# Four conditioning chunks of the second mixer move from TensorE to VectorE, and four are made during the first feed-forward stage

## The chip, the core and the metric

The kernel runs on one NeuronCore of a Trainium2 chip. The core has five engines with instruction streams of their own: TensorE (PE in the profile; PEld is its weight load), VectorE (DVE), ScalarE (ACT), GpSimd (POOL) and SyncE (SP), which here only issues DMAs. Each engine works through its stream in order and waits on semaphores for the others. The metric is the device time of one execution in microseconds (us): 676.04 us for the kernel before, the median of 3 runs (675.55 to 677.71).

## The reference

Two layers (L = 2) work on 256 tokens of width 1024 in float32. In each layer a conditioning vector c gives, through a matrix of 1024 x 6144, a shift, a scale and a gate for the mixer and the same for the feed-forward part:

```python
c_act = jax.nn.silu(c)
for l in range(DEPTH):
    mod = (c_act @ w_ada[l] + b_ada[l])[:, None, :]
    shift_a, scale_a, gate_a, shift_f, scale_f, gate_f = jnp.split(mod, 6, axis=-1)
    h = rmsnorm(x, g_mix_pre[l]) * (1.0 + scale_a) + shift_a
    y = hybrid_mixer(h, w_in[l], ...)           # three kinds of attention, then w_out
    x = x + gate_a * rmsnorm(y, g_mix_post[l])
    h = rmsnorm(x, g_ffn_pre[l]) * (1.0 + scale_f) + shift_f
    x = x + gate_f * rmsnorm(swiglu(h, w_gate_up[l], w_down[l]), g_ffn_post[l])
```

The conditioning is a product of one vector with a matrix: 48 MB of weights for both layers, and little arithmetic. Everything else is matrix products over 256 tokens, and row norms and softmaxes between them.

## The kernel before

**Stages.** The program runs mixer 0, feed-forward 0, mixer 1, feed-forward 1. Between two of them lies a boundary: the post-norm of one stage and the pre-norm of the next, token tile by token tile (two tiles of 128 tokens, t = 0 and 1). In a boundary ScalarE squares and sums a row (`junk`), VectorE adds the sums (`rs`), GpSimd takes the power -1/2, VectorE scales (`yg`, `x`, `xn`), TensorE transposes (`xT`), ScalarE applies scale and shift (`hv`, line 384), and VectorE splits the result into a leading part (`h1aH`, line 386) and a rest (`h1aL`, line 387).

**Products.** Every product is made of three, of leading parts and rests. So each weight piece of 128 x 1024 is loaded (`raw`, four buffers), rounded by ScalarE (`wh`, line 102) and subtracted by VectorE (`wl`, line 103; six buffers of each).

**Conditioning.** For each of the four norms there are 12 chunks of 256 columns: chunks 0 to 7 hold shift and scale of 128 features each (`scale_step`), and four more the gates (`gate_step`). A chunk is 1 MB, loaded in two halves (`adaw`, line 257) into a ring of four half buffers, so that the load of a half waits until the half four places earlier has been used. A chunk is made in one of two ways (`ada_chunk`): on VectorE, by one multiply-and-sum instruction for each half (line 266, shown as CUSTOM_DVE in the trace), or on TensorE, by 8 products (`adap`, line 274), a copy by ScalarE (`adasb`, line 277), two transposes (`adac`, line 286) and a sum by VectorE (line 287). `on_dve` says which. For the second norm of layer 1 (`ab11`) VectorE takes chunks 1, 3, 5 and 7, and TensorE takes 0, 2, 4 and 6.

**Where chunks stand.** `todo` is a list of such steps, and `fill()` takes the next one off it. Mixer 1 has 12 steps (4 gates, 8 scales), called from its start, from its latents and after each of its eight pairs of heads. Feed-forward 0 has 12 steps (4 gates of its own, 8 scales for the first norm of layer 1), one for each tile f of the hidden width from f = 4 on (f runs from 0 to 21). In the feed-forward stage a chunk is also ordered behind the weight piece before it (`order_after`).

**What sets the order.** The tile framework places each engine's instructions by a model of durations and priorities when the program is built, so an instruction can stand far from where it is written: in the kernel before, the loads of mixer 1's gates and of its scale chunks 0 to 2 are issued, and the gates and chunk 1 made, before feed-forward 0 has ended. On the chip that order is fixed. All loads go through SP's one queue: a load that waits for its buffer holds up every load behind it.

Of the kernel before, what the change touches and what calls it, by code (L numbers as in the profile page):

```python
# [14 lines left out]
L = 2  # L15
D = 1024
# [17 lines left out]
MIX_DVE = (3, 5, 6, 7), (1, 3, 5, 7)  # L34


def on_dve(l, which, j):
    """which engine takes the products of a chunk (j < 8: scale and shift, then gates) with the conditioning"""
    if which == 1 and j < KC:
        return j in MIX_DVE[l]  # L40
    return j >= KC or l > 0
# [3 lines left out]
def block_kernel(ctx, tc, A, out):  # L45
# [47 lines left out]
    def chain(i):  # L93
        """products of the start: in the order in which they are written"""
# [10 lines left out]
    def prep(key):  # L105
# [14 lines left out]
        for u in range(nh):  # L120
# [8 lines left out]
            # beside the norms of the layer boundary: small pieces, so that a norm waits less  # L129
# [16 lines left out]
    def mm3(ps, w, x, start, stop):  # L146
        # weights stationary
# [4 lines left out]
    def tokens(ps, h, ts_, w, halves=False):  # L152
        """one token tile over all of D, w: (high, low) per chunk"""
# [4 lines left out]
        # the low parts of h arrive last  # L158
# [9 lines left out]
    def mm3t(ps, x, w, start, stop):  # L168
        # tokens stationary
# [10 lines left out]
    # columns: per norm and chunk b_ada of shift, b_ada of scale (32) | 32:40 g_mix_pre | 40:48 g_ffn_pre  # L180
    #          48:50 g_q_lat | 50:51 g_kv_lat | 51:59 g_group
    #          59:91 per norm b_ada of the gate, g_mix_post | g_ffn_post
# [17 lines left out]
    # the tensor engine's clock is up by the time that the first weights arrive  # L200
# [4 lines left out]
    # silu(c), repeated over 32 columns  # L205
# [8 lines left out]
    # and as a row on every partition  # L214
# [8 lines left out]
    # T5 bias of the causal tile, as a Toeplitz read of the per-distance values  # L223
    mobab = const.tile([P, 4, S], F32, name="mobab")

    def t5_bias():
# [12 lines left out]
        # a copy for each partition: row p is read from its element 127 - p on  # L239
# [20 lines left out]
    def ada_chunk(l, which, j):  # L260
        raws = loaded.pop((l, which, j), None) or ada_load(l, which, j)
        if on_dve(l, which, j):
            # features on partitions
# [16 lines left out]
    def ada_columns(l, which, j, sb, dst):  # L280
        """sums of a chunk, features on partitions"""
# [17 lines left out]
    def rows_of(sb, tag):  # L299
        """the columns of sb as one row on every partition, through a scratch in DRAM"""  # L300
# [29 lines left out]
    def scale_step(l, which, kc, sb=None):  # L330
        if kc == 0:
            ABs[l, which] = act.tile([P, KC, 2], F32, tag="ab", bufs=3, name=f"ab{l}{which}")
        ada_scale(l, which, ABs[l, which], kc, ada_chunk(l, which, kc) if sb is None else sb)

# [502 lines left out]
    def ffn(l, hH, hL, norm, fill, silu_set):  # L837
# [63 lines left out]
        for f in range(NF):  # L901
            if f >= HEADF:
# [3 lines left out]
                if f >= 4:  # L906
                    fill()
# [207 lines left out]
```

## Time and profile before

| what | value |
|---|---|
| runs | 676.04 us median of 3 (675.55 to 677.71) |
| profiled execution, span from first to last instruction | 675.6 us |
| TensorE busy | 639.2 us (95%) |
| VectorE busy | 451.4 us (67%) |
| ScalarE busy | 366.5 us (54%) |
| GpSimd busy | 51.3 us (8%) |
| moved by DMA | 155.29 MB, mean 230 GB/s |
| conditioning halves made by VectorE (line 266) | 64, 77.7 us |

The page has no time of the profiled execution other than its span, which lies within 0.1 us of the fastest run and 0.4 us below the median. Feed-forward 0 lies at about 176 to 350 us, the boundary to mixer 1 at 350 to 367 us, mixer 1 at 367 to 470 us. Busy shares of the whole span say little here: what counts is which engine the others wait for in each of these stretches, and where TensorE has gaps.

### The profile page before, as it was taken

Reading aid. Unit: us, or ns where it says so; the run is one execution under the profiler, and the core shown is the slowest. Engines: PE = TensorE matmul, PEld = TensorE weight load, DVE = VectorE, ACT = ScalarE, POOL = GpSimd, SP = SyncE. Lnnn points to the kernel's source line nnn. Section 1 sums busy time; section 2 is a strip of 40 time slices with the busy share of each in tenths; the row PEclk is TensorE's granted clock in tenths of the full one; section 3 lists DMA queues with packets and bytes.
Section 4 is the critical chain, followed back from the end, with each engine's and each line's share of the span. In section 5 each row is a group of like instructions: output and inputs, shape, how many; then the busy total and the mean of one; then the engine's idle time right before and its main releaser. Section 6 shows DMA issues by size and latency. Waiting matters only on the chain.

```text
span 675.6 us, 12108 instructions
## 1 busy us (share of the span) xinstructions
PE 639.2 (95%) x4543; PEld 565.5 (84%) x4543; DVE 451.4 (67%) x969; ACT 366.5 (54%) x758; POOL 51.3 (8%) x90
## 2 busy tenths in 40 slices
PE   8989759999999999999999999899899999999996
PEld 6878647667999999999978988668799999999994
DVE  2458277888777777798658765775878755555543
ACT  5447427768654444444458665786764444444431
POOL 1000021421000000000001010240100000000000
PEclk9999979999999999999999999899999999999999
DMA  9968595886478898898844875551558676555511
GB/s 320 407 227 286 168 322 179 281 289 215 147 245 316 310 328 304 313 337 290 313 139 147 296 230 184 201 182 64 187 195 276 219 236 184 185 181 185 184 62 63
DMA packets 44410, 155.29 MB, mean 230 GB/s; under 512 B 5136, under 2 KB 6464, under 8 KB 44352
## 3 DMA queue, kind: packets, MB, share of 16 engines
q1 hardware_dynamic: 44352, 154.52, 67.4%
q8 instruction: 36, 0.59, 0.3%
q14 instruction: 22, 0.18, 0.1%
HBM read 152.64 MB, written 1.86 MB: 229 GB/s over the span
## 4 chain that ended last, share of the span: by engine, by line
PE 74%; DVE 9%; DMA 8%; ACT 3%; issue 2%; POOL 2%; SPq 1%; DVEq 0%; POOLq 0%; ACTq 0%
PE gu L148 11%; PE gu L149 11%; PE gu L150 11%; PE y L171 8%; PE y L172 8%; PE y L170 8%; DMA adaw<-in_w_ada_dram 4%; DVE wl L103 3%; PE adap L274 2%; PE o L478 2%; DMA scr<-band 2%; ACT wh L102 1%; DMA raw_b<-in_w_b_dram 1%; POOL rs L343 1%; DVE adaw L266 1%
## 5 line engine op out<-in xcount | busy, mean ns | idle before, releaser
L103 DVE TENSOR_TENSOR wl<-raw_gu,wh 128x1024 fp32r<-128x1024 f32 (+1 forms) x100 | 108.5, 1096 | 68.8 <-ACT wh L102 68.5
L102 ACT ACTIVATE wh<-raw_gu 128x1024 fp32r<-128x1024 f32 (+1 forms) x100 | 94.4, 958 | 92.6 <-PE gu L149 64.5
L148 PE MATMUL gu<-h0fL,wh 128*128 128x256 f32 x304 | 86.2, 283 | 0.0
L148 PE MATMUL gu<-h1fL,wh 128*128 128x256 f32 x304 | 86.2, 283 | 0.0
L149 PE MATMUL gu<-h1fH,wh 128*128 128x256 f32 x304 | 86.0, 283 | 0.0
L149 PE MATMUL gu<-h0fH,wh 128*128 128x256 f32 x304 | 86.0, 283 | 0.0
L150 PE MATMUL gu<-h0fH,wl 128*128 128x256 f32 x304 | 86.0, 283 | 0.0
L150 PE MATMUL gu<-h1fH,wl 128*128 128x256 f32 x304 | 86.0, 283 | 0.0
L266 DVE CUSTOM_DVE_ANT_0 adaw<-adaw,crow 128x1024 f32<-128x1024 f32 x64 | 77.7, 1229 | 8.4 <-DMA adaw<-in_w_ada_dram 8.4
L102 ACT ACTIVATE wh<-raw_dn 128x1024 fp32r<-128x1024 f32 x44 | 46.7, 1062 | 56.8 <-issue 34.7
L171 PE MATMUL y<-wh,hid 128*128 128x512 f32 x176 | 69.6, 396 | 0.0
L170 PE MATMUL y<-wh,hid 128*128 128x512 f32 x176 | 69.5, 396 | 0.0
L172 PE MATMUL y<-wl,hid 128*128 128x512 f32 x176 | 69.5, 395 | 0.0
L103 DVE TENSOR_TENSOR wl<-raw_dn,wh 128x1024 fp32r<-128x1024 f32 x44 | 53.7, 1224 | 23.3 <-ACT wh L102 23.1
L149 PEld LDWEIGHTS gu<-h0fH,wh 128*128 128x128 f32 x304 | 58.3, 192 | 0.4
L149 PEld LDWEIGHTS gu<-h1fH,wh 128*128 128x128 f32 x304 | 58.3, 192 | 0.4
L148 PEld LDWEIGHTS gu<-h1fL,wh 128*128 128x128 f32 x304 | 58.2, 192 | 0.4
L148 PEld LDWEIGHTS gu<-h0fL,wh 128*128 128x128 f32 x304 | 58.2, 192 | 0.4
L150 PEld LDWEIGHTS gu<-h1fH,wl 128*128 128x128 f32 x304 | 58.3, 192 | 0.0
L150 PEld LDWEIGHTS gu<-h0fH,wl 128*128 128x128 f32 x304 | 58.3, 192 | 0.0
L343 POOL TENSOR_TENSOR rs<-rs,mhalf 128x1 f32<-128x1 f32 x16 | 11.0, 687 | 439.1 <-DVE rs L342 439.1
L172 PEld LDWEIGHTS y<-wl,hid 128*128 128x128 f32 x176 | 33.0, 188 | 8.0
(331 smaller groups left out, 1483.1 us busy)
## 6 DMA issues: line engine op xcount, KB each, us to landing
adaw<-in_w_ada_dram SPq DMA_DIRECT2D x96, 512.0 KB, 6.6
raw_gu<-in_w_gu_dram SPq DMA_DIRECT2D x88, 512.0 KB, 4.7
raw_dn<-in_w_dn_dram SPq DMA_DIRECT2D x44, 512.0 KB, 4.7
raw_out<-in_w_out_dram SPq DMA_DIRECT2D x16, 512.0 KB, 5.0
raw_b<-in_w_b_dram SPq DMA_DIRECT2D x12, 512.0 KB, 5.7
raw_a<-in_w_a_dram SPq DMA_DIRECT2D x8, 448.0 KB, 10.0
raw_uq<-in_w_uq_dram SPq DMA_DIRECT2D x4, 512.0 KB
raw_vm<-in_w_vm_dram SPq DMA_DIRECT2D x4, 512.0 KB, 5.0
```

What stands on the lines that cost most here:

```text
L102: ACT.activation(dst_h, src, AF.Copy)
L103: return DVE.tensor_tensor(dst_l, src, dst_h.bitcast(F32), op=ALU.subtract)
L148: chain(PE.matmul(ps, w[0], x[1], start=start, stop=False))
L149: chain(PE.matmul(ps, w[0], x[0], start=False, stop=False))
L150: chain(PE.matmul(ps, w[1], x[0], start=False, stop=stop))
L170: PE.matmul(ps, x[1], w[0], start=start, stop=False)
L171: PE.matmul(ps, x[0], w[0], start=False, stop=False)
L172: PE.matmul(ps, x[0], w[1], start=False, stop=stop)
L266: i = DVE.tensor_tensor_reduce(out=raws[u], in0=raws[u], in1=crow, op0=ALU.mult, op1=ALU.add, scale=1.0, scalar=0.0, accum_out=sb[:, u:u + 1])
L274: chain(PE.matmul(ps[32 * g:32 * g + 32, :], crep[:, kc, :], raws[kc // 4][:, g * 256:(g + 1) * 256], start=kc < 4, stop=kc >= 4, tile_pos ...
L343: POOL.tensor_tensor(r, r, mhalf, op=ALU.pow)
L478: PE.matmul(o[64 * u:64 * u + 64, lo:lo + P], v[:, u * 64:(u + 1) * 64], ps[u][:, i * P:(i + 1) * P], start=start, stop=stop, tile_positio ...
```

## The change

`on_dve` now answers yes for every chunk of layer 1, so chunks 0, 2, 4 and 6 of the second norm leave TensorE; the host lays out their weights for VectorE. Chunks 0 to 3 (`FFN_MADE`) leave the list of mixer 1 and are appended to that of feed-forward 0, behind the 12 steps that it had. Feed-forward stages call `fill()` from f = 3 on and not from f = 4. `scale_step` makes its result tile at the first chunk it meets and not at chunk 0. Comments and docstrings were dropped as well, so that line numbers shift by 2 (line 266 becomes 268, 103 becomes 105); those lines of the diff are left out here.

```diff
-MIX_DVE = (3, 5, 6, 7), (1, 3, 5, 7)
+MIX_DVE = 3, 5, 6, 7
+
+FFN_MADE = 0, 1, 2, 3
 
 def on_dve(l, which, j):
-    if which == 1 and j < KC:
-        return j in MIX_DVE[l]
+    if l == 0 and which == 1 and j < KC:
+        return j in MIX_DVE
     return j >= KC or l > 0
...
     def scale_step(l, which, kc, sb=None):
-        if kc == 0:
+        if (l, which) not in ABs:
             ABs[l, which] = act.tile([P, KC, 2], F32, tag="ab", bufs=3, name=f"ab{l}{which}")
...
                 up(f)
                 while turns:
                     turns.pop(0)()
-                if f >= 4:
+                if f >= 3:
                     fill()
...
-        todo += [(gate_step, l, 0, j) for j in range(4)] + [(scale_step, l, 1, j) for j in range(KC)]
+        todo += [(gate_step, l, 0, j) for j in range(4)]
+        todo += [(scale_step, l, 1, j) for j in range(KC) if l == 0 or j not in FFN_MADE]
...
         if l + 1 < L:
             todo.extend((scale_step, l + 1, 0, j) for j in range(KC))
+            todo.extend((scale_step, l + 1, 1, j) for j in FFN_MADE)
```

VectorE's stream at the end of feed-forward 0 and the start of the boundary, before: `hid` is the rest of the last hidden tile, `yg` and `rs1` the post-norm of token tile 0.

```order
L103 TENSOR_TENSOR hid_1936<-ffv_3950,hid_1936 128x256
L405 TENSOR_TENSOR yg_4125<-y_2503,gp_2689 128x512
L342 TENSOR_SCALAR rs1_4133<-s2_4127 128x1
L405 TENSOR_TENSOR yg_4126<-y_2504,gp_2689 128x512
L411 SCALAR_TENSOR_TENSOR x_75<-yg_4125,rs1_4133,x_75 128x512
```

The same place in the changed kernel; adaw_4629 and adaw_4630 are the halves of chunk 4, adaw_4789 is the first half of chunk 5 (the ISA row after each is the read of its sum).

```order
L105 TENSOR_TENSOR hid_1936<-ffv_3987,hid_1936 128x256
L268 ISA adaw_4629,adasum_4633<-adaw_4629,crow_110 128x1024
L268 ISA adasum_4633 128x1
L268 ISA adaw_4630,adasum_4633<-adaw_4630,crow_110 128x1024
L268 ISA adasum_4633 128x1
L407 TENSOR_TENSOR yg_4162<-y_2512,gp_2622 128x512
L296 TENSOR_TENSOR ab11_3444<-adasum_4633,first_73 128x2
L298 SCALAR_TENSOR_TENSOR ab11_3444<-ab11_3444,first_73 128x1
L268 ISA adaw_4789,adasum_4793<-adaw_4789,crow_110 128x1024
L268 ISA adasum_4793 128x1
L344 TENSOR_SCALAR rs1_4170<-s2_4164 128x1
L407 TENSOR_TENSOR yg_4163<-y_2513,gp_2622 128x512
```

Three halves now stand between the last hidden tile and the first `rs1` of the norm, where there were none.

VectorE's stream in the pre-norm of token tile 0, before, with `yg` and `rs1` of token tile 1 behind it:

```order
L386 CAST h1aH_4075<-hv4_4154 128x4x128
L387 TENSOR_TENSOR h1aL_4076<-hv4_4154,h1aH_4075 128x4x128
L386 CAST h1aH_4075<-hv4_4168 128x4x128
L387 TENSOR_TENSOR h1aL_4076<-hv4_4168,h1aH_4075 128x4x128
L405 TENSOR_TENSOR yg_4175<-y_2511,gp_2689 128x512
L342 TENSOR_SCALAR rs1_4183<-s2_4177 128x1
```

The same place in the changed kernel; adaw_4790 is the second half of chunk 5.

```order
L388 CAST h1aH_4112<-hv4_4191 128x4x128
L268 ISA adaw_4790,adasum_4793<-adaw_4790,crow_110 128x1024
L268 ISA adasum_4793 128x1
L389 TENSOR_TENSOR h1aL_4113<-hv4_4191,h1aH_4112 128x4x128
L388 CAST h1aH_4112<-hv4_4205 128x4x128
L407 TENSOR_TENSOR yg_4212<-y_2520,gp_2622 128x512
L389 TENSOR_TENSOR h1aL_4113<-hv4_4205,h1aH_4112 128x4x128
L344 TENSOR_SCALAR rs1_4220<-s2_4214 128x1
```

A half stands between leading part and rest of the first four feature tiles, which the first product of mixer 1 reads.

TensorE's stream in mixer 1 ahead of the third pair of heads, before: `qkp` is a projection, `kn` and `qp` are keys and queries of the pair, and `adap` and `adac` make chunk 2.

```order
L150 MATMUL qkp_4862<-h1aH_4075,wl_4449 128x256
L274 MATMUL adap_4916<-adaw_4912,crep_108 32x256 x4
L274 MATMUL adap_4916<-adaw_4913,crep_108 32x256 x4
L148 MATMUL kn_4933<-kvL_4081,wh_4103 128x256
L149 MATMUL kn_4933<-kvH_4080,wh_4103 128x256
L150 MATMUL kn_4933<-kvH_4080,wl_4104 128x256
L148 MATMUL qp_4939<-cqL_4083,wh_4087 128x256
L149 MATMUL qp_4939<-cqH_4082,wh_4087 128x256
L150 MATMUL qp_4939<-cqH_4082,wl_4088 128x256
L148 MATMUL qp_4939<-cqL_4083,wh_4095 128x256
L286 MATMUL adac_4927<-first_73,adasb_4925 128x128 x2
L149 MATMUL qp_4939<-cqH_4082,wh_4095 128x256
```

The same place in the changed kernel:

```order
L152 MATMUL qkp_4886<-h1aH_4112,wl_4486 128x256
L150 MATMUL kn_4945<-kvL_4118,wh_4140 128x256
L151 MATMUL kn_4945<-kvH_4117,wh_4140 128x256
L152 MATMUL kn_4945<-kvH_4117,wl_4141 128x256
L150 MATMUL qp_4951<-cqL_4120,wh_4124 128x256
L151 MATMUL qp_4951<-cqH_4119,wh_4124 128x256
L152 MATMUL qp_4951<-cqH_4119,wl_4125 128x256
L150 MATMUL qp_4951<-cqL_4120,wh_4132 128x256
L151 MATMUL qp_4951<-cqH_4119,wh_4132 128x256
```

The ten instructions are gone and nothing stands in their place; it is the same for the other three chunks.

## Rows read from the trace of the kernel before

**Rows 1.** Windows by stage: us, busy (count) of each engine, clock, DMA.

```profile
core 0: us, PE busy (x) PEld busy (x) DVE busy (x) ACT busy (x) POOL busy (x), PEclk, DMA share, GB/s
176.00:350.00 174.00, 174.00 (x1225) 163.00 (x1225) 132.28 (x217) 80.83 (x115) 0.55 (x1) 1.00 0.82 285
350.00:367.00 17.00, 15.35 (x88) 13.08 (x86) 14.94 (x35) 13.76 (x38) 2.32 (x3) 1.00 0.54 166
367.00:470.00 103.00, 97.88 (x726) 81.97 (x727) 69.28 (x220) 71.93 (x195) 19.08 (x35) 0.98 0.57 191
```

**Rows 2.** The same window for tile adap, then tile adac alone.

```profile
367.00:470.00 103.00, 4.28 (x64) 1.67 (x64) 1.50 (x4) 0.98 0.57 191
367.00:470.00 103.00, 1.64 (x8) 0.86 (x8) 0.66 (x4) 0.98 0.57 191
```

**Rows 3.** Chain that ended last, mixer 1: start us, us, what.

```profile
412.70 1.00 PE adap L274 x16
414.72 0.22 PE adac L286 x2
```

**Rows 4.** Timeline of PE, mixer 1: start, us, form, [idle before <-releaser].

```profile
403.24 0.44 PE L451 MATMUL pt<-first,e 128*128 128x128 f32 x2 [0.39 <-POOL e L445]
...
426.83 0.77 PE L458 MATMUL s<-kx,qx 128*128 128x128 f32 x2 [1.53 <-DVE qx L761]
...
439.54 0.43 PE L478 MATMUL o<-pts,vc 128*64 128x128 f32 x2 [0.38 <-ACT pts L453]
...
447.71 0.50 PE L170 MATMUL y<-wh,o1L 128*128 128x512 f32 x1 [0.87 <-DVE o1L L103]
```

**Rows 5.** Windows of mixer 1 in which the clock fell.

```profile
426.00:428.00 2.00, 1.17 (x4) 1.10 (x5) 2.00 (x4) 1.95 (x5) 0.00 (x0) 0.69 0.35 109
428.00:430.00 2.00, 2.00 (x10) 1.26 (x10) 1.63 (x6) 0.30 (x1) 0.00 (x0) 0.50 0.68 221
```

**Rows 6.** Timeline of DVE, mixer 1: two conditioning halves.

```profile
418.83 1.23 DVE L266 CUSTOM_DVE_ANT_0 adaw<-adaw,crow 128x1024 f32<-128x1024 f32 x1 [2.22 <-DMA adaw<-in_w_ada_dram]
...
443.62 1.36 DVE L266 CUSTOM_DVE_ANT_0 adaw<-adaw,crow 128x1024 f32<-128x1024 f32 x1
```

**Rows 7.** Window of the last pairs of mixer 1.

```profile
436.00:450.00 14.00, 12.33 (x103) 7.64 (x103) 13.93 (x71) 12.47 (x45) 8.34 (x16) 1.00 0.82 279
```

**Rows 8.** Page, group of the conditioning on VectorE.

```profile
L266 DVE CUSTOM_DVE_ANT_0 adaw<-adaw,crow 128x1024 f32<-128x1024 f32 x64 | 77.7, 1229 | 8.4 <-DMA adaw<-in_w_ada_dram 8.4
```

**Rows 9.** Timeline of DVE, end of feed-forward 0 and boundary.

```profile
344.86 0.69 DVE L405 TENSOR_TENSOR yg<-y,gp 128x512 f32<-128x512 f32 x1 [2.65 <-ACT junk L356]
347.72 0.21 DVE L342 TENSOR_SCALAR rs<-s 128x1 f32<-128x1 f32 x1 [2.16 <-ACT junk L356]
...
366.18 0.43 DVE L386 CAST h1aH<-hv 128x512 fp32r<-128x512 f32 x1 [0.64 <-ACT hv L384]
```

**Rows 10.** Windows of the end of feed-forward 0.

```profile
288.00:305.00 17.00, 17.00 (x121) 15.95 (x120) 16.22 (x30) 7.82 (x11) 0.00 (x0) 1.00 0.96 341
305.00:344.00 39.00, 39.00 (x263) 35.88 (x262) 26.35 (x41) 17.61 (x24) 0.00 (x0) 1.00 0.84 294
344.00:350.00 6.00, 6.00 (x27) 4.82 (x26) 2.84 (x6) 2.88 (x7) 0.55 (x1) 1.00 0.02 6
```

**Rows 11.** DMA issues from 312 to 344 us: count, KB each, median us to landing.

```profile
adaw<-in_w_ada_dram SPq DMA_DIRECT2D x6, 512.0 KB, 7.2
```

**Rows 12.** Timeline of PE, boundary and start of mixer 1.

```profile
353.35 1.10 PE L380 MATMUL xT<-first,xn 128*128 128x128 f32 x8 [0.63 <-DVE xn L377]
...
356.92 0.43 PE L170 MATMUL vps<-wh,h1aL 128*128 128x420 f32 x1
...
367.39 0.46 PE L170 MATMUL vps<-wh,h1aL 128*128 128x420 f32 x1 [0.92 <-DVE h1aL L387]
...
386.24 0.33 PE L567 MATMUL latT<-first,lat 128*128 128x128 f32 x1 [0.23 <-DVE kvL L571]
```

**Rows 13.** Timeline of DVE, start of mixer 1.

```profile
381.85 2.55 DVE L103 TENSOR_TENSOR wl<-raw_b,wh 128x512 fp32r<-128x512 f32 x4 [1.31 <-ACT wh L102]
```

## The prediction

> **What bounds the kernel now.** I read the windows by stage first. In feed-forward 0 TensorE is busy for 174.00 of 174 us and VectorE for 132.28 [rows 1]: there the weight products are the bound, and VectorE has 42 us to spare. In mixer 1 TensorE is busy for 97.88 of 103 us; what is not busy lies in gaps that VectorE, ScalarE and GpSimd release [rows 1, 4]. In the boundary between them VectorE is busy for 14.94 of 17 us and TensorE waits for the norm [rows 1, 12]. So an instruction taken from TensorE in mixer 1 counts nearly in full, one added to VectorE in feed-forward 0 counts nothing while it keeps up, and one added to VectorE in the boundary counts wherever it stands in the chain of the norm. All three happen here.
>
> **Taken from TensorE.** The four chunks have 4.28 us of `adap` and 1.64 us of `adac` [rows 2]. Busy times of TensorE overlap, since ends are modelled; the chain of waits counts 1.00 + 0.22 = 1.22 us for one chunk [rows 3], 4.9 us for four. The ends are thus 4.9 and 5.9; I take 5.2, nearer to the chain, which doesn't count overlaps twice. In the order nothing takes the place of these instructions, and the products around them don't wait for the conditioning.
>
> **Taken from VectorE in mixer 1.** The halves of chunks 3, 5 and 7 stand between the softmax instructions there; one waited 2.22 us for its load, with the next pair's softmax queued behind it, and another ran for 1.36 us [rows 6] in a stretch in which VectorE was busy for 13.93 of 14 us and ScalarE for 12.47 [rows 7]. In the changed order no half stands behind the first softmax of mixer 1. The four larger gaps of TensorE there are 0.39 + 1.53 + 0.38 + 0.87 = 3.2 us [rows 4]. VectorE released two of them, and the others hang on softmaxes that it feeds; ScalarE, nearly as full, keeps some of them open. Between 0 and 3.2 I take 1.8. [...] Sum of the gains: 5.2 + 1.8 + 0.6 = 7.6 us; ends 4.9 and 5.9 + 3.2 + 1.4 = 10.5.
>
> **Added beside feed-forward 0.** The page's mean of one half is 1229 ns [rows 8]. Chunks 0 to 3 take f = 15 to 18; the gates of mixer 1, which stood there, slide towards the end. Before, 1 of the 8 scale chunks was made there; now it is 4, so the stage gets three chunks more, 6 x 1.23 = 7.4 us for VectorE's 42 us of slack: hidden, except at the very end, where the rest of the last weight piece and the last hidden tile come behind the halves of the last gate. For this I take 0.7 us, from nothing to 2.5, the two halves.
>
> **Moved into the boundary.** Only chunks 0 to 3 go beside the feed-forward stage. Chunks 4 to 7, all on VectorE now, come next in the list, and the order puts their eight halves where the norm and the first weights of mixer 1 are.
> Three (chunk 4, first half of 5) stand between the last hidden tile and the first `rs` of the norm. VectorE idled there for 2.65 + 2.16 = 4.8 us [rows 9], and 3 x 1.23 = 3.7 us fit, if the loads are there. A load took 7.2 us from issue to landing [rows 11]. Both loads of chunk 4 stand in SP's queue behind pieces of `c` that wait for buffers of the last `dn` pieces, so I put their issue at about 339 and their landing at 346 us, when `yg` is due at 344.86. An `rs` due at 347.72 then comes at 349 to 350: 1.8 us late; from 0.4 (all loads in time) to 4.5 (below, first rival). TensorE's cover is thin: it waited 0.63 us for `xn` as it was [rows 12].
> The second half of chunk 5 stands between `h1aH` and `h1aL` of token tile 0, for which the first product of mixer 1 waits [rows 12]. The delay of 1.2 us is 0.6 for tile 1, as the products of tile 0 cover part of it. The first half of chunk 6 stands in front of `h1aH` of tile 1, where VectorE idled for 0.64 us [rows 9]: 1.23 - 0.64 = 0.6 late, and TensorE had waited there already [rows 12]. Together 1.1 (rounded down); ends 0 and 2 x 1.23.
> The second half of 6 and both of 7 stand between the `wl` of the first projections: 3.7 us. VectorE idled 1.31 us there for ScalarE and a load [rows 13], and TensorE waited 0.23 us for what follows, `kvL` [rows 12]. But a late VectorE also frees `raw` buffers later. I take 0.9; ends 0 and 3.7.
> Losses: 0.7 + 1.8 + 1.1 + 0.9 = 4.5 us, less 0.3 since a late end of the stage hides a late norm: 4.2. Ends: 0.4 and 2.5 + 4.5 + 2.5 + 3.7 = 13.2, which don't add up, as each delay gives the next load time; I keep 10.
>
> **Sum.** -7.6 + 4.2 = -3.4 us from a span of 675.6, to 672.2. The page has only that span; the median of the runs, 676.04, is 0.44 above it, so the runs should give 672.6 us. The clause for f = 3 only starts conditioning one tile earlier in both feed-forward stages; TensorE is gapless there [rows 1], and I count nothing.
>
> [...] The loads of the end of feed-forward 0 are what decides the term of 1.8. The row: 341 GB/s at a share of 0.96 was the most in a long window, 294 at 0.84 where the chunks now go [rows 10]. [...]
>
> **Rivals.**
> *Slower, by late loads in the boundary.* From 312 to 344 us six halves were issued [rows 11]; the changed order has the four gates, chunk 4 and half of 5 there, 11 halves. Five more of 0.52 MB at 341 GB/s are 7.7 us, and the free share from 305 to 344 is 0.16 x 39 = 6.2 us [rows 10], so the last half lands 1.5 us late plus whatever SP's queue adds. From a landing of chunk 5 at about 352 us on, `rs` is 4.5 us late. TensorE then stands still long enough for its clock to fall as it did after 1.53 us [rows 5], at 1.0 us in each tile, 2.0 in all. Sum: -6.5 (fewer gaps closed, as mixer 1 starts late on its weights) + 0.7 + 4.5 + 1.1 + 0.9 + 2.0 = +2.7: 678.7. For it: the gaps of SP's queue, and VectorE without slack behind f = 18. Against: from 344 to 350 DMA was idle, share 0.02 [rows 10].
> [...]
> *No change.* Mixer 1 is held by the chain of softmax, exponent and transposes, so that TensorE's 5.2 us turn into waits. For it: ScalarE's 12.47 of 14 us, VectorE's 13.93 [rows 7]. Against: that stretch is a seventh of the mixer and loses two halves itself. Half of the 5.2, 1.2 of gaps and clock: -3.8 + 4.2 = +0.4: 676.4.
> *Faster than forecast.* Loads in time, gaps closed: -5.5 - 3.0 - 1.0 + 1.5 = -8: 668.0. Against it: the order as shown.
>
> **How the numbers follow.** Forecast 0.50, its own range 670 to 675; slower 0.20; no change 0.18; faster still 0.12. A measurement of this kernel can tell 0.3%, 2.0 us, from no change. Faster than 674.0: 0.12, and 0.47 of the forecast's 0.50, 0.59. Slower than 678.1: 0.6 of the rival's chance, spread around 678.7, and its large tail, together 0.17. Within: 0.24. The range 668 to 679.5 leaves out the better half of the last case, and the rival's upper third.
>
> **What would show it.** In the profile after: no `adap` from 367 us on; the gaps of VectorE in front of `yg` and `rs` filled, and what ended the rest (a load of `adaw`, or the squares of ScalarE); the first `xT` at about 354 to 356 us, and the first product of mixer 1 at 359 to 361; from there to the first product of `y` some 7 us less than before. Feed-forward 0 must stay without gaps up to 343 us. The prediction is wrong if that stage gets longer by more than 2 us, if the boundary loses over 7, or if mixer 1 from its first product to its last is shortened by under 4.

## The result, and the profile after

| | before | after |
|---|---|---|
| median, us (lowest to highest) | 675.79 (674.87 to 677.71), 4 runs | 684.62 (684.27 to 686.93), 4 runs |
| ratio of after to before | | 1.0124, 95% interval 1.0102 to 1.0145 |
| profiled span, us | 675.6 | 685.1 |
| mean granted clock | 0.988 | 0.976 |

The changed kernel is 1.2% slower, where I forecast half a per cent faster. Of the forecast's own signs of being wrong one is met beyond doubt: mixer 1 got longer. Boundary and start of the mixer lost 6.98 us, at the edge of the 7 that I had named. The first `xT` at 355.86 and the first product of mixer 1 at 360.45 us (below) lie in the ranges that I gave, but by luck: feed-forward 0 began 0.84 us earlier in this execution, and without that both are outside. From that product to the first product of `y` it is 93.79 us (360.45 to 454.24), 3.0 more than the 90.79 before (356.92 to 447.71 [rows 4, 12]), where I expected some 7 less.

The windows of the three stages, changed kernel (us; busy time and count of PE, PEld, DVE, ACT and POOL; clock, DMA share, GB/s), which answer to [rows 1]:

```profile
176.00:350.00 174.00, 173.09 (x1216) 161.50 (x1215) 139.27 (x234) 79.79 (x114) 0.00 (x0) 1.00 0.88 305
350.00:367.00 17.00, 13.42 (x60) 11.40 (x59) 15.86 (x34) 11.80 (x31) 2.73 (x4) 0.90 0.71 239
367.00:470.00 103.00, 93.01 (x646) 79.32 (x645) 63.02 (x204) 68.06 (x189) 17.87 (x34) 0.92 0.41 137
```

VectorE's halves moved as the order said (139.27 us beside feed-forward 0, 63.02 in mixer 1). But in the boundary TensorE's clock is 0.90, and in mixer 1 it is 0.92 instead of 0.98.

To see where the time went I follow one chain of milestones, counted from the first gate-and-up product of feed-forward 0 in the same trace. TensorE's timeline, kernel before: that product, the first score of mixer 1, and the first `xT` behind the mixer.

```profile
164.43 0.38 PE L163 MATMUL gut<-wh,h0fH 128*128 128x256 f32 x1 [0.59 <-DVE h0fH L386]
...
393.24 0.67 PE L458 MATMUL s<-kx,qx 128*128 128x128 f32 x4
...
474.91 1.07 PE L380 MATMUL xT<-first,xn 128*128 128x128 f32 x8 [0.80 <-DVE xn L377]
```

The same in the changed kernel, with the lines that answer to [rows 4, 12]:

```profile
163.59 0.39 PE L165 MATMUL gut<-wh,h0fH 128*128 128x256 f32 x1 [0.59 <-DVE h0fH L388]
...
343.62 0.50 PE L172 MATMUL y<-wh,hid 128*128 128x512 f32 x1 [0.90 <-DVE hid L105]
...
355.86 1.10 PE L382 MATMUL xT<-first,xn 128*128 128x128 f32 x8 [1.72 <-DVE xn L379]
...
360.45 0.43 PE L172 MATMUL vps<-wh,h1aL 128*128 128x420 f32 x1 [1.86 <-DVE h1aL L389]
...
371.69 0.46 PE L172 MATMUL vps<-wh,h1aL 128*128 128x420 f32 x1 [0.99 <-DVE h1aL L389]
...
392.38 0.47 PE L569 MATMUL latT<-first,lat 128*128 128x128 f32 x1 [2.06 <-DVE kvL L573]
...
399.64 0.57 PE L460 MATMUL s<-kx,qx 128*128 128x128 f32 x3
...
438.87 0.44 PE L453 MATMUL pt<-first,e 128*128 128x128 f32 x2 [1.09 <-POOL e L447]
...
448.98 0.70 PE L420 MATMUL st<-acc,shp 128*128 128x256 f32 x2 [1.37 <-DVE acc L486]
...
454.24 0.80 PE L172 MATMUL y<-wh,o1L 128*128 128x512 f32 x1 [1.25 <-DVE o1L L105]
...
484.28 0.96 PE L382 MATMUL xT<-first,xn 128*128 128x128 f32 x7 [0.81 <-DVE xn L379]
```

| milestone, us from the first gate-and-up product | before | after | later by |
|---|---|---|---|
| first `xT` of the boundary | 188.92 | 192.27 | 3.35 |
| first product of mixer 1, token tile 0 | 192.49 | 196.86 | 4.37 |
| the same, token tile 1 | 202.96 | 208.10 | 5.14 |
| the `latT` that waits for `kvL` | 221.81 | 228.79 | 6.98 |
| first score | 228.81 | 236.05 | 7.24 |
| first `xT` behind mixer 1 | 310.48 | 320.69 | 10.21 |

Feed-forward 0 began 0.84 us earlier and what follows the last milestone is 0.1 us longer, so that 9.5 us remain, the difference of the spans. The profiled execution of the changed kernel is the slowest of its four (686.93 us), so this is more than the 8.8 us between the medians. There are two losses: 7.0 us up to the latents, and 3.2 us from there on, where I had forecast 7.6 us of gain.

The second is seen in the windows from the first score to the first `xT` behind the mixer, before and after:

```profile
393.24:474.91 81.67, 76.37 (x548) 61.05 (x547) 55.78 (x186) 57.77 (x157) 18.63 (x34) 0.98 0.53 178
```

```profile
399.64:484.28 84.64, 76.95 (x491) 61.88 (x492) 47.48 (x156) 56.31 (x154) 17.59 (x34) 0.92 0.26 86
```

TensorE has 57 instructions fewer (54 of them three chunks, 4.41 us of its busy time; chunk 0 lies ahead of the first score) and is busy 0.58 us longer. VectorE has 8 us less to do. The windows of the last pairs, changed kernel, show why:

```profile
446.00:448.00 2.00, 0.77 (x3) 0.34 (x3) 1.05 (x8) 2.00 (x9) 1.67 (x4) 1.00 0.00 0
448.00:450.00 2.00, 1.02 (x4) 0.49 (x4) 1.13 (x8) 1.40 (x7) 0.84 (x3) 1.00 0.00 0
450.00:452.00 2.00, 1.42 (x11) 1.14 (x10) 0.88 (x2) 2.00 (x9) 0.80 (x2) 0.60 0.00 0
452.00:454.00 2.00, 1.00 (x4) 0.50 (x3) 0.86 (x6) 1.69 (x6) 0.31 (x1) 0.50 0.00 0
454.00:456.00 2.00, 1.76 (x5) 0.99 (x6) 1.99 (x6) 0.74 (x3) 0.96 (x2) 0.50 0.00 0
456.00:458.00 2.00, 2.00 (x14) 1.55 (x12) 0.70 (x3) 0.95 (x5) 0.68 (x2) 0.50 0.00 0
```

No engine is full up to 450 us but ScalarE for a moment: the softmaxes of the last pairs follow one another, and TensorE works for 1.79 of 4 us. Then its clock falls to 0.50, and stays there when the products of `y` have come.

### The profile page after: what moved, and what is told of

Its sections match the earlier page's. It is cut to its first block, busy times and chain, and to the rows that moved or that the text cites. A ratio compares the mean times of both kernels' runs of the same rounds, so it can differ in the third digit from the quotient of the medians.

```text
span 685.1 us, 11964 instructions
## 1 busy us (share of the span) xinstructions
PE 641.9 (94%) x4471; PEld 567.7 (83%) x4471; DVE 458.9 (67%) x981; ACT 364.4 (53%) x754; POOL 50.4 (7%) x90
## 3 DMA queue, kind: packets, MB, share of 16 engines
HBM read 152.64 MB, written 1.86 MB: 226 GB/s over the span
## 4 chain that ended last, share of the span: by engine, by line
PE 73%; DVE 11%; DMA 8%; ACT 3%; POOL 2%; issue 2%; SPq 1%; DVEq 0%; POOLq 0%; ACTq 0%
PE gu L150 10%; PE gu L151 10%; PE gu L152 10%; PE y L173 7%; PE y L174 7%; PE y L172 7%; DMA adaw<-in_w_ada_dram 5%; DVE wl L105 4%; PE o L480 2%; DVE adaw L268 2%; PE adap L276 2%; PE pt L453 2%; PE s L462 1%; DMA scr<-band 1%; PE s L460 1%
## 5 line engine op out<-in xcount | busy, mean ns | idle before, releaser
L268 DVE CUSTOM_DVE_ANT_0 adaw<-adaw,crow 128x1024 f32<-128x1024 f32 x72 | 87.2, 1222 | 4.9 <-DMA adaw<-in_w_ada_dram 4.8
L174 PE MATMUL y<-wl,hid 128*128 128x512 f32 x176 | 69.5, 395 | 0.0
L172 PEld LDWEIGHTS y<-wh,hid 128*128 128x128 f32 x176 | 33.1, 188 | 8.7 <-DVE hid L105 1.6
```

Of the source, the lines that this page charges most:

```text
L172: PE.matmul(ps, x[1], w[0], start=start, stop=False)
L174: PE.matmul(ps, x[0], w[1], start=False, stop=stop)
L268: i = DVE.tensor_tensor_reduce(out=raws[u], in0=raws[u], in1=crow, op0=ALU.mult, op1=ALU.add, scale=1.0, scalar=0.0, accum_out=sb[:, u:u + 1])
```

## The experiments

Theory A: the eight halves of chunks 4 to 7, which the new order puts into the boundary and the start of mixer 1, cost the first 7 us. Theory B: TensorE's conditioning work lay between softmaxes that wait anyway, and kept its clock up; without it the waits stay and the clock falls. A rival to B is the order: without these instructions the scheduler also set TensorE's last scores and transposes in another order. All ratios are to the kernel before, run beside each experiment. The milestones are from each run's one profile, counted as above.

| run | ratio (95% interval) | first `xT` | first score | first score to `xT` behind the mixer | clock there |
|---|---|---|---|---|---|
| before | 1 | 188.92 | 228.81 | 81.67 | 0.98 |
| after | 1.0124 (1.0102 to 1.0145) | 192.27 | 236.05 | 84.64 | 0.92 |
| 1 without chunks 4 to 7 | 1.0033 (1.0014 to 1.0053) | 190.83 | 229.26 | 82.78 | 0.94 |
| 2 halves held | 1.0080 (1.0051 to 1.0110) | 190.61 | 229.70 | 86.37 | 0.90 |
| 3 before, without TensorE's chunks | 1.0076 (1.0033 to 1.0118) | 193.15 | 231.86 | 81.29 | 0.96 |
| 4 unused products | 1.0072 (1.0053 to 1.0091) | 192.48 | 234.08 | 79.60 | 1.00 |
| 5 their order alone | 1.0096 (1.0071 to 1.0121) | 192.66 | 234.07 | 83.33 | 0.94 |
| 6 the products in the old order | 1.0097 (1.0060 to 1.0134) | 192.99 | 234.79 | 80.79 | 1.00 |
| 7 chunks 4 and 6 on TensorE | 1.0030 (1.0007 to 1.0052) | 190.49 | 229.38 | 82.98 | 0.98 |
| 8 the same, two gates later | 1.0002 (0.9982 to 1.0023) | 189.05 | 227.32 | 83.92 | 0.96 |
| 9 before, without TensorE's chunks, held | 1.0053 (1.0031 to 1.0076) | 188.88 | 227.15 | 85.69 | 0.94 |
| 10 the same, unused products | 0.9995 (0.9971 to 1.0019) | 188.89 | 227.82 | 81.64 | 0.98 |
| 11 all on VectorE, late gates, products | 0.9989 (0.9965 to 1.0013) | 189.07 | 227.33 | 81.28 | 1.00 |
| 12 run 8 with products | 0.9974 (0.9948 to 1.0001) | 189.06 | 227.36 | 82.37 | 0.98 |

### 1. Without chunks 4 to 7

```diff
-        todo += [(scale_step, l, 1, j) for j in range(KC) if l == 0 or j not in FFN_MADE]
+        todo += [(scale_step, l, 1, j) for j in range(KC) if l == 0]
+        if l:
+            DVE.tensor_copy(ABs[1, 1][:, 4:8, :].rearrange("p a b -> p (a b)"), ABs[1, 0][:, 4:8, :].rearrange("p a b -> p (a b)"))
```

> The changed kernel with chunks 4 to 7 of layer 1's second norm left out altogether (no loads, no halves; the scale and shift of these features are copied from the first norm, so the output is not the reference's). The changed kernel measured 684.6 us, the one before 675.8. Theory A (the eight halves that the new order puts into the boundary and the start of mixer 1 cost the 6.1 us by which the first latent transpose is late): that transpose comes at about 386 to 388 us instead of 392.4, and the time falls to about 678, more if the late weights also widened the gaps behind it. Theory B (the last pairs of mixer 1 lack TensorE's conditioning work between their softmaxes, so that gaps widen and the clock falls): the stretch from the first latent transpose to the end of mixer 1 stays at about 87 us (84.0 before, 87.5 after), so that 2.5 to 3.5 us of the loss remain whatever the boundary does. If both hold: 678 to 679. If the boundary alone were the cause: 670 to 673, since TensorE then has 5 us less to do than in the kernel before.

Theory A held, theory B in part. The first score comes 6.8 us earlier than in the changed kernel, within 0.5 us of the kernel before; the stretch behind it is still longer than before, with a clock of 0.94. But from the `latT` to the first `xT` behind the mixer it is 88.64 us, as much as before (88.67) and not as much as in the changed kernel (91.90), which B expected. So theory A has the size of the first loss, and taking it away leaves the kernel 0.3% slower than before, with even less to compute: TensorE's four chunks are gone, and the mixer is no shorter. Most of the 0.3% is the first `xT`, 1.9 us late, which run 8 puts down to feed-forward 0.

### 2. The halves held behind the latents

```diff
                 if last.get("ffn"):
                     order_after(i, last["wl"])
+                elif l == 1 and which == 1 and j < KC:
+                    order_after(i, last["lat"])
```

> The changed kernel, with the eight halves of chunks 4 to 7 ordered behind the last latent split of mixer 1, so that norm and boundary stand as in the kernel before and the halves stand among the first pairs' softmaxes. Theory A: the first xT returns to 353.4 to 354.5 us and the first latent transpose to about 386 to 387 (392.4 in the changed kernel), 5 to 6 us gained; of these the softmax stretch takes back what eight halves of 1.23 us cost there, 0 to 3 us. Time 679 to 682. Theory B says the same of the boundary, and that the stretch from the latent transpose to the end of mixer 1 gets no shorter than 87 us. If the boundary's delay was only idle time that mixer 1 had in any case (rival): the time stays at 684 to 685.

The first score gained 6.35 us; the softmaxes among which the halves then stood took 1.7 us more than in the changed kernel, at a clock of 0.90. Counted from feed-forward 0, the first `xT` came at 190.61 against 188.92 before, with nothing added to the norm, and the `latT` that waits for `kvL` at 224.01 against 221.81: later than expected. The 1.7 us at `xT` come from feed-forward 0 (run 8). By its ratio the time is 681.2 us (1.0080 x 675.79), inside the 679 to 682 expected.

### 3. The kernel before without TensorE's chunks

```diff
-        todo += ... [(scale_step, l, 1, j) for j in range(KC)]
+        todo += ... [(scale_step, l, 1, j) for j in range(KC) if l == 0 or j in MIX_DVE[1]]
+        if l:
+            ABs[1, 1] = act.tile([P, KC, 2], F32, tag="ab", bufs=3, name="ab11")
+            DVE.tensor_copy(ABs[1, 1], ABs[1, 0])
```

> The kernel before, with the four chunks of layer 1's second norm that TensorE makes (0, 2, 4, 6) left out altogether, their loads too (scale and shift of these features come from the first norm, so the output is not the reference's). VectorE gets nothing more; its chunks 1, 3, 5, 7 stay in mixer 1. If TensorE's work counts in full, as I forecast: 676 - 5.2 = 670 to 671. Theory B (that work was filler between softmaxes): no gain or a loss, 675 to 679, with wider gaps of TensorE and a granted clock under 1.00 in the last pairs, and the stretch from the first latent transpose to the end of mixer 1 at 84 us or more. Rival (no change by waits alone): the gaps grow by about 5 us, the clock stays at 1.00, 675 to 677.

Slower than before although four chunks are gone, by more than either theory said (1.0076 x 675.79 is 680.9 us), but not a clean test: the list moved up, VectorE's chunks slid into feed-forward 0, and the first `xT` came 4.2 us later. TensorE's timeline at its end:

```profile
345.91 0.50 PE L170 MATMUL y<-wh,hid 128*128 128x512 f32 x1 [2.46 <-DVE hid L103]
```

The window from the first score to the first `xT` behind the mixer:

```profile
396.36:477.65 81.29, 73.65 (x492) 59.69 (x492) 47.44 (x156) 56.41 (x154) 17.62 (x34) 0.96 0.28 90
```

This stretch has neither TensorE's three chunks nor a half on VectorE, and is only 0.4 us shorter than before, where three quarters of 5.2 us, 3.9, should have gone. TensorE's idle time there rose from 5.3 to 7.6 us, and the clock fell from 0.98 to 0.96. From the `latT` on it is 87.16 us against 88.67 before: shorter, though by far less than forecast, and not longer as theory B had it. Run 9 repeats it without the slide.

### 4. Unused products between the last pairs

```diff
+KEEP = 3, 4, 5, 6, 7
...
             project_more(i + 1)
             fill()
+            if l and i in KEEP:
+                kw = pm("keep").rearrange("p (a b) -> p a b", a=4)
+                for _ in range(5):
+                    PE.matmul(kw, zero, zero[:, None, :].to_broadcast([P, 4, P]), start=True, stop=True)
```

> The changed kernel, with five TensorE products of 128x512 written behind each of pairs 3 to 7 of mixer 1, of zeros with zeros, whose result nobody uses. 25 products, at about 0.25 us 6 us of work more, as much as the four chunks had. [...] Theory B with the chain alone (the last pairs wait for softmaxes whatever TensorE does): 684 to 685, the fillers lie in the gaps. Rival (TensorE is the bound there): 688 to 691.

The window from the first score on; the 25 products are 7.2 us of TensorE's busy time:

```profile
397.17:476.77 79.60, 76.70 (x516) 62.04 (x517) 47.59 (x156) 56.34 (x154) 18.31 (x34) 1.00 0.29 95
```

TensorE has 25 products more than in the changed kernel, is busy 0.25 us less, and is done 5.0 us earlier: without the products its 491 instructions were busy for about 69.5 us, in the changed kernel for 76.95. The clock of the stretch is 1.00 instead of 0.92, and by its ratio the time is 680.7 us (1.0072 x 675.79), under the 684 to 685 of the waits alone, which agrees with theory B by the clock. The first score came 2.0 us earlier too (in run 5 as well), which the products' work can't have done: the first of them stands at 433 us. And the products also moved the scheduler's order of the last scores and transposes; runs 5 and 6 take the two apart.

### 5 and 6. The order without the products, the products without the order

In both, TensorE's instructions from the sixth pair to the end of the mixer are chained in a written order: in run 5 that of run 4, without its products; in run 6 that of the changed kernel, around the products. REC holds these instructions as they are written in the source, and the numbers (their first ones, of run 5, stand here) say in which order they go.

```diff
+ORDER = [0, 1, 2, 3, 4, 5, 6, 7, 8, 9, 17, 10, 18, 11, 12, 13, 14, 15, 19, 20, 21,
...
+    for a, b in zip(ORDER, ORDER[1:]):
+        order_after(REC[b], REC[a])
```

> The changed kernel without the unused products, but with TensorE's instructions from the sixth pair of mixer 1 to the end of the mixer in exactly the order that the kernel with the unused products has there (its scores all stand ahead of the transposes of the pair before, where the changed kernel has two of the four behind them). This and the next kernel split what the unused products changed: 25 products of work, and this order. Changed kernel against the one before: 1.0124; with the unused products 1.0072. Filler theory (the products keep TensorE busy between the softmaxes, and its clock up): 1.010 to 1.013, and the windows from 440 to 460 us still show a clock under 0.8. Order theory (the changed order makes TensorE wait for transposes with ready scores behind them): 1.006 to 1.008, clock 1.00.

> The changed kernel with the 25 unused products in mixer 1, and with TensorE's other instructions from the sixth pair on held in exactly the changed kernel's order. Filler theory: 1.006 to 1.009 against the kernel before, the clock 1.00 from 440 to 460 us. Order theory: 1.012 to 1.020 (the waits are those of the changed kernel, and 6 to 7 us of products are added, part of it in the waits).

The same windows, run 5 first:

```profile
397.57:480.90 83.33, 75.73 (x491) 61.11 (x492) 47.40 (x156) 56.75 (x154) 17.80 (x34) 0.94 0.28 91
```

```profile
399.99:480.78 80.79, 76.93 (x517) 62.48 (x517) 47.84 (x156) 56.41 (x154) 18.11 (x34) 1.00 0.29 94
```

In this stretch the products are worth 3.7 to 3.9 us (84.64 to 80.79, 83.33 to 79.60) and the order 1.2 to 1.3 (84.64 to 83.33, 80.79 to 79.60); the clock follows the products (0.92 and 0.94 without them, 1.00 with them in either order) and not the order. In the whole time the two runs came out alike, each just outside the filler theory's range (by 0.0004 and 0.0007) and further from the order theory's (0.0016 and 0.0023). Run 6 waited 1.64 us at the end of feed-forward 0 in its profile, and the intervals are 0.5% to 0.7% wide. So B's mechanism is shown in the stretch, by one profile each, with the order as a smaller second part; the shares in the median stay open.

### 7 and 8. Two candidates

Run 7 holds chunks 5 and 7 as run 2 does and gives 4 and 6 back to TensorE, behind the fifth and seventh pair. Run 8 also makes two gates behind the latents, and chunk 5 beside feed-forward 0 in the place of one.

```diff
+BACK = 4, 6
...
+            if l and i in BACK:
+                scale_step(1, 1, i)
...
-        todo += [(gate_step, l, 0, j) for j in range(4)]
+        todo += [(gate_step, l, 0, j) for j in range(4 - 2 * l)]
+        todo += [(lambda: None,)] * l
         todo += [(scale_step, l, 1, j) for j in range(KC) if l == 0 or j not in FFN_MADE + BACK]
+        todo += [(gate_step, l, 0, j) for j in range(4 - 2 * l, 4)]
```

> A candidate: chunks 0 to 3 beside feed-forward 0 as in the changed kernel, chunks 5 and 7 on VectorE but ordered behind the last latent split, and chunks 4 and 6 back on TensorE, behind the fifth and the seventh pair, where they stand between the last softmaxes. By both theories together it loses neither the boundary (6 us of the changed kernel's loss) nor the clock in the last pairs; what is left of the loss is the end of feed-forward 0 (0.9 to 1.5 us), against 2 chunks of 1.3 us less of TensorE and three chunks fewer of VectorE in mixer 1: 0.994 to 1.002 of the kernel before. If TensorE's two chunks are not enough to keep the clock: 1.003 to 1.006.

> The same candidate with the last two gate chunks of mixer 1 made behind the latents as well, and chunk 5 in the place of one of them beside feed-forward 0: one chunk less in the crowded end of feed-forward 0, one more on VectorE among the first pairs. If the 1.3 to 1.7 us by which the first xT is late even with chunks 4 to 7 out of the boundary come from too many conditioning chunks at the end of feed-forward 0, the first xT comes at 189 to 190 us from the first gate-and-up product (188.9 before, 190.6 to 190.8 with the eight halves held or left out), and the time is 1 us under that of the other candidate: 0.993 to 1.001. If they come from elsewhere, the two candidates are equal.

Run 7 came out at the foot of the range for a clock that doesn't hold (1.003), though its clock did hold: 1.00 from 440 to 460 us. Its first `xT` is 1.57 us late, and its waits in the stretch are 1.2 us more than before. Run 8 came out inside its range. With one chunk fewer at the end of feed-forward 0 the first `xT` came at 189.05 and not 190.49, so the lateness there was the crowd of chunks. Run 8 reaches its first score 1.5 us before the kernel before, and loses it again to waits, 1.27 us among the first pairs and this one in the last, after which the clock was 0.66 from 440 to 450 us:

```profile
438.92 0.48 PE L423 MATMUL st<-acc,shp 128*128 128x256 f32 x1 [1.39 <-DVE acc L489]
```

### 9 and 10. TensorE's term by itself

Run 9 is run 3 with VectorE's chunks 3, 5 and 7 ordered behind the latents and TensorE's last pairs in the order of the kernel before. Run 10 adds the five products of run 4 behind pairs 3 and 5 (counted from 0), where chunks 4 and 6 had stood.

```diff
+                elif l == 1 and which == 1 and j in (3, 5, 7):
+                    order_after(i, last["lat"])
...
+KEEP = 3, 5
```

> The kernel before with TensorE's four chunks (0, 2, 4, 6) of layer 1's second norm left out, loads too (scale and shift of these features come from the first norm, so the output is not the reference's). Unlike in the earlier run without them, VectorE's chunks 3, 5 and 7 are ordered behind the last latent split, so that none of them slides into feed-forward 0, and TensorE's instructions from the sixth pair on stand in the order of the kernel before. This is the term of 5.2 us alone. My forecast's reading: 0.991 to 0.993 of the kernel before. Filler theory: what goes comes back as waits and a lower clock, at least for the two chunks in the last pairs; from the first score to the first xT behind the mixer 80 to 82 us (81.7 before), 0.996 to 1.001 overall.

> The same kernel, with five unused products of zeros (128x512, about 1.4 us) at each of the two places in the last pairs where chunks 4 and 6 stood. Filler theory: no slower than without them, although TensorE has 2.8 us more to do, and the clock is 1.00 from 430 to 460 us: 0.993 to 0.998. If TensorE's work counts in full: 2.8 us slower than without them.

The windows from the first score to the first `xT` behind the mixer, run 9, then run 10:

```profile
392.50:478.19 85.69, 74.59 (x492) 61.04 (x492) 52.61 (x170) 56.97 (x154) 21.61 (x34) 0.94 0.35 120
```

```profile
392.47:474.11 81.64, 74.16 (x504) 60.71 (x502) 52.79 (x170) 56.77 (x154) 21.25 (x34) 0.98 0.37 125
```

The longest wait of TensorE, run 9, then run 10:

```profile
441.45 0.87 PE L59 MATMUL pt<-first,e 128*128 128x128 f32 x3 [2.72 <-POOL e L465]
```

```profile
441.53 0.52 PE L60 MATMUL pt<-first,e 128*128 128x128 f32 x3 [2.71 <-POOL e L466]
```

Windows of the last pairs, run 9, then run 10:

```profile
440.00:446.00 6.00, 3.62 (x20) 2.79 (x20) 2.73 (x15) 3.88 (x16) 2.04 (x5) 0.72 0.00 0
446.00:454.00 8.00, 5.71 (x24) 4.00 (x25) 3.05 (x9) 4.83 (x15) 2.54 (x4) 0.63 0.01 2
454.00:462.00 8.00, 8.00 (x52) 6.10 (x51) 2.27 (x6) 3.62 (x10) 0.00 (x0) 0.94 0.00 0
```

```profile
440.00:446.00 6.00, 4.47 (x23) 3.42 (x25) 2.47 (x14) 4.18 (x16) 2.12 (x5) 0.72 0.00 0
446.00:454.00 8.00, 7.42 (x57) 5.27 (x54) 3.70 (x13) 5.23 (x17) 2.07 (x4) 1.00 0.01 2
454.00:462.00 8.00, 8.00 (x44) 6.42 (x44) 3.70 (x9) 5.70 (x14) 0.00 (x0) 1.00 0.00 0
```

Runs 9 and 10 are the cleanest pair. Their fronts are nearly the same (first score at 227.15 and 227.82), and so is the wait at 441.5 us (2.72 and 2.71 us, for GpSimd's `e`), after which the clock falls in both (0.72 from 440 to 446 us). With the products TensorE is back at the full clock from 446 us on (1.00 to 462 us); without them it falls again (0.63 from 446 to 454 us). Giving useless work back, 10 products with 4.00 us of busy time in the trace, made the kernel as fast as before: the intervals of the two runs don't overlap.

Run 9 against the kernel before is less clean. Two more things differ: six halves stand among the first pairs (a wait of 1.28 us at 403.31, 0.39 before [rows 4]), and only TensorE's last pairs are held in the old order, not the other engines; the wait of 2.72 us is not in the kernel before. So the 0.5% is not the price of the missing work alone. Runs 3 and 9 together show no gain worth naming from taking away the three chunks behind the first score. Chunk 0, ahead of it, is a gain: from the `latT` to the first score it is 7.00 us before and 5.69 in run 9, 1.3 us less, about the 1.22 of [rows 3]. In the changed kernel the same stretch took 7.26 us, at a clock of 0.59 and 0.55 over the first four (the windows at the latents, below), so that not even this gain was seen there.

Both runs came out worse than I had expected for the filler theory (0.996 to 1.001 and 0.993 to 0.998). The second group of products comes at 442.22 us, behind the wait at 441.5 us, and doesn't bridge it; the clock behind it is 0.72 in run 10 too.

### 11 and 12. A version that beats both?

Run 11 is run 8 with all eight chunks on VectorE (`BACK = ()`) and the products of run 4; run 12 is run 8 with `KEEP = 3, 5, 6`.

> A candidate: all eight chunks on VectorE as in the changed kernel; the last two gates and chunks 5 to 7 ordered behind the latents, so that nothing stands in the boundary and the end of feed-forward 0 has one chunk less; and the 25 unused products between the last pairs. From the runs so far: first score about 227.5 to 229.5 us behind the first gate-and-up product (227.3 in the candidate with the gates, 229.7 with the eight halves held), then 79.6 to 81 us to the first xT behind the mixer as with the unused products, 307 to 310.5 in sum against 310.5 before: 0.995 to 1.000. If the ten halves among the first pairs' softmaxes hold TensorE up: 1.000 to 1.004.

> The candidate with the gates (chunks 4 and 6 on TensorE), and five unused products behind pairs 3, 5 and 6. Without them it was at 1.0002 with a clock of 0.66 from 440 to 450 us. Filler theory: clock 1.00 there, from the first score to the first xT 80 to 82 us instead of 83.9: 0.995 to 0.998. If the wait in front of the group sum, 1.39 us, is what costs, not the clock: 0.999 to 1.003.

Both are clearly better than the changed kernel. Run 12, the fastest, is 0.26% under the kernel before, with an interval that ends at 1.0001: that it beats the kernel before is likely, not shown. Its clock from 440 to 460 us was 1.00, as expected, but the stretch took 82.37 us, not 80 to 82. Run 11's ratio lies in its range too, its stretch of 81.28 just above the 79.6 to 81.

## Why the prediction was wrong

**Taken from TensorE, 5.2 us: the step that failed.** I wrote that "nothing takes the place of these instructions, and the products around them don't wait for the conditioning". Both halves are true and the conclusion is false. The products around them wait for softmaxes, and three of the four chunks stood among those waits. In place of the 3.9 us that these three should have given, run 3 has 0.4, with 2.3 us more idle time of TensorE and a lower clock (0.96 against 0.98). Run 9 has a loss of 0.5%, about 3.6 us, part of it by its held halves and by the order of the other engines; and run 10 shows that work at two of these places is worth more than it costs (1.0053 to 0.9995). Only chunk 0, ahead of the first score, counted as I had said: 1.3 us in run 9. I had taken the 97.88 busy of 103 us [rows 1] as a sign that TensorE is the bound; a busy share doesn't tell work that others wait for from work that fills a wait.

**Gaps, 1.8 us, and clock, 0.6 us: wrong in sign.** VectorE's halves left as I said, but in the stretch from the first score on TensorE's idle time rose from 5.3 to 7.7 us (81.67 - 76.37, 84.64 - 76.95), because the cover was gone; runs 5 and 6 put a smaller part down to the order. A clock of 0.92 over 84.64 us is 6.8 us of full clock lost, idle time included, against 0.02 x 81.67 = 1.6 before: 5 us more. The busy time says the same: 4.41 us of chunks went, and it rose by 0.58. No run shows the 0.6 us that the forecast's sum has for the clock (1.4 at its end); the runs showed the clock lower in its place, 0.92 here and 0.96 in run 3. [rows 4, 5] had shown a clock of 0.69 and 0.50 behind a gap of 1.53 us; I priced it where it was, and not where the removed work would open others. Only the rival "slower" let the clock fall, and in the boundary alone, where it was 0.90. It was the last pairs that I should have asked about: runs 6 and 10 raise the clock by products alone, with TensorE's order held (0.92 to 1.00, 0.94 to 0.98).

**Boundary and start of mixer 1, 4.2 us: right mechanism, too small.** The loss was 7.0 us, under the end of 10 that I kept. VectorE's timeline in the changed kernel, answering to [rows 9]: the halves of chunk 4, the first of chunk 5, and the first `rs`.

```profile
345.63 1.23 DVE L268 CUSTOM_DVE_ANT_0 adaw<-adaw,crow 128x1024 f32<-128x1024 f32 x1 [2.07 <-DMA adaw<-in_w_ada_dram]
...
346.89 1.23 DVE L268 CUSTOM_DVE_ANT_0 adaw<-adaw,crow 128x1024 f32<-128x1024 f32 x1
...
349.22 1.23 DVE L268 CUSTOM_DVE_ANT_0 adaw<-adaw,crow 128x1024 f32<-128x1024 f32 x1 [0.23 <-DMA adaw<-in_w_ada_dram]
...
350.37 0.21 DVE L344 TENSOR_SCALAR rs<-s 128x1 f32<-128x1 f32 x1
```

The load of chunk 4 came at 345.6 us (I had put 346), and `rs` at 350.37, or 3.5 us late by the milestones' clock, where I had 1.8: the three halves and a `yg` simply follow one another behind the late load. My own landing would have given that, 346 + 3 x 1.23 + 0.69 = 350.4, had I not left out the `yg` and written 349 to 350. The first `xT` lost 3.35 us (forecast 0.7 + 1.8 - 0.3), the pre-norms 1.8 up to token tile 1 (1.1), the start of the mixer 1.8 (0.9). Behind two of these gaps, 1.86 us at 360.45 and 2.06 us at 392.38 us, the clock fell as well, to 0.50 from 362 to 364 us and to 0.59 and 0.55 from 392 to 396; the windows at the latents:

```profile
392.00:394.00 2.00, 1.62 (x5) 1.35 (x6) 1.23 (x7) 0.73 (x2) 0.00 (x0) 0.59 0.92 324
394.00:396.00 2.00, 2.00 (x8) 1.44 (x8) 0.63 (x2) 1.30 (x3) 0.00 (x0) 0.55 0.91 350
```

**Beside feed-forward 0: right, inside its ends.** The stage has no gap up to 343 us; one of 0.90 us follows, for `hid`, where I had 0.7 and an end of 2.5. In other runs it is up to 1.64 us (run 6), and the first `xT` 1.6 to 1.9 us late with the norm left as it was (runs 1, 2 and 7). Run 8 showed that this tail is the crowd of chunks.

**Two readings that were off and moved little.** I called 341 GB/s [rows 10] the most in a long window; the profile's own second slice, 17 to 34 us, has 407. It did not harm the term of 1.8: chunk 4 was issued at 338.96 us and landed at 345.6, as I had reckoned. And I put the runs 0.44 us above the span, while every run on record lasts 1.7 to 2.1 us longer than the span of the same execution; that shifts both kernels alike.

**The rivals.** "No change" had the mechanism, waits in the place of work, but only for half of it, and still counted gaps and clock as gains. "Slower" had the boundary nearly right, and still counted 6.5 us of gain in the mixer. None let the mixer itself get longer.

## What to carry to other kernels

Before work is counted as a gain, look at what stands on either side of it in that engine's stream: if the next instruction waits for another engine, the removed work was cover, and only what it had over that wait can be gained. On TensorE such cover also held the clock here (0.92 in the changed kernel, 1.00 in run 6 with unused products in the place of the work), so removing it can cost more than it saves; a few unused products in its place are a cheap test. And where work moves to, the order decides, not the stage with the slack: the halves with no place beside feed-forward 0 landed in the norm.

## What the runs showed of the hardware

The clock fell with no long stop. In the last pairs of the changed kernel no wait is over 1.4 us, TensorE was busy for 1.79 of the 4 us from 446 at a clock of 1.00, and from 452 us on the granted clock was 0.50, even where TensorE was busy for 1.76 and 2.00 of 2 us again. A product of 128x512 took 0.80 us there (454.24), and 0.50 before [rows 4].

A first, shorter fall had come at 440 us, where TensorE was busy for 1.13 of the 2 us before:

```profile
440.00:442.00 2.00, 2.00 (x10) 1.25 (x11) 1.50 (x8) 1.96 (x9) 0.93 (x2) 0.54 0.69 213
```

The wait in front of it, 1.09 us at 438.87 us, is for GpSimd. Its scaling of a 128x256 block took 1.44 us, and a later one 0.48:

```profile
437.38 1.44 POOL L447 TENSOR_SCALAR e<-e,ri 128x256 f32<-128x256 f32 x1
...
439.15 0.48 POOL L447 TENSOR_SCALAR e<-e,ri 128x256 f32<-128x256 f32 x1
```

VectorE ran a subtraction with two inputs (`wl`, 1.27 us from 437.20) beside the first. Whether the one made the other longer no run shows. In the kernel before, a conditioning half stood in the same way beside such a scaling: 1.36 us at 443.62 [rows 6], and the scaling of 443.89 us took 1.44 instead of 0.48.
